# Byte addresses of TensorE's operands, and attention by pairs of heads

## The chip, the cores and the metric

The kernel runs on one core of a Trainium2 chip. The time is that of one execution of the whole program on the device, in microseconds (us); lower is better. Three runs were timed, and one execution was profiled.

## The reference

Two transformer blocks over 256 tokens of width 1024, in float32. The first block has two layers, each with a half-step feed-forward (FFN, width 2816, SwiGLU), a mixer (gated convolution, pooling, attention) and another FFN; layer 0 runs also on 256 context tokens, so most of its products have 512 token columns. Its attention has 8 heads of 64:

```
def ffn_sublayer(x, m, i, g, w1, w2):
    return x + HALF_STEP * m[:, 3 * i + 2, None] * swiglu(mod_norm(x, m, i, g), w1, w2)
...
s = jnp.concatenate([s_loc.reshape(B, NA_HEADS, nj, NA_QC, n_loc), s_ctx], axis=-1)
p = jax.nn.softmax(s, axis=-1).astype(v.dtype)
```

An image token attends to a neighbourhood among the 256 image tokens and to all 256 context tokens (512 scores a row); a context token to the 256 context tokens alone. The second block has retention, a sparse attention of 8 heads of 64 (two branches: all tokens up to the query, and a few compressed ones), and a layer of 16,384 experts of which each token takes 16 for each of 8 heads.

## The kernel before

Everything is kept with features on the 128 partitions and tokens along the row. A weight matrix comes from memory in units of 128x1024 (`Stream`): SyncE loads a unit into a `raw` buffer, and `Stream.split` (L238 to L242) makes of it two float32r halves, high and low, in an `hl` buffer: ScalarE copies the high half, VectorE or GpSimd subtracts. The buffers are taken in turn: `hl0` to `hl3`, two more in the FFNs (`hm`), one more in the second block (`hx`). The activations are split too: `Hh` and `Hl`, and `G` (high and low) behind the gate. `mm3` (L284 to L286) then makes three matmuls for each 128x128 block: high weight by high activation, high by low, low by high. In each, TensorE loads the weight block (128 columns) and streams 512 or 256 token columns past it. In three places (`winv`, `win2r`, and `wup` at L1813) the roles are turned: `Hh` or `Hl` is loaded and 512 columns of the unit are streamed.

All of these tiles lie at fixed bytes of a partition, one after the other in the order in which `run` allocates them. The built program gives these addresses modulo 256 bytes: X, Hh, Hl, hl0 and hl1 stand at 128; G, hl2 and hl3 at 96; hm at 0; hx at 128. Two more buffers, cut from the second halves of Hh and Hl for the expert units, stand at 128. Steps from block to block within a tile are multiples of 256 bytes, so each of its blocks has the tile's address modulo 256.

Attention in the first block (`attention`, L1028) is a generator; an item is one kind of query (image x or context c), one head h and one block qt of 128 queries. `mixer` calls it after every second block column k of its projections in layer 0, and after every fourth in layer 1, so one step lies between 6 or 12 matmuls of L284 to L286. In a step, for an item i, it issues: the softmax of item i+2 (`soft`), the division of item i+1 (`scale`), the scores of item i+3 (`score`, L1043, one float32 matmul over the 64 partitions of the head: heads with even number on partitions 0 to 63, odd ones on 64 to 127), the transposes of item i (`trans`, L1074, blocks of 128) and the products with V of item i-1 (`pv`, L1088, 64 weight columns, so the output goes to 64 PSUM partitions: 0 to 63 for even heads, 64 to 127 for odd ones). A float32 matmul is two passes, and the trace counts each as one. TensorE takes its instructions in the order written, so this order decides which matmuls are next to each other. Before the first step three scores are issued in a row:

```
        for i in range(3):
            prep(i)
            score(i)
        soft(0)
```

The scores go to three PSUM banks in turn (`sb`). Layer 0 has 32 items, 16 x and 16 c, layer 1 has 16 x. The sparse attention of the second block (`nsa`, L1340 on) has the same pipeline with 16 items (j, g, qt): L1393 scores (two matmuls of 128 columns for qt 0, of 256 for qt 1), L1429 transposes, L1440 and L1443 products (three matmuls for qt 0, five for qt 1).

Of the kernel before, what the change touches and what calls it, by code (L numbers as in the profile page):

```python
# [26 lines left out]
NSA = 68  # L27
MIX_LINS = (8, 9, 0, 10, 4, 11, 2, 6, 7, 1, 5, 3), (8, 9, 6, 10, 7, 11, 0, 4, 2, 1, 5, 3)
# [149 lines left out]

class Stream:
# [45 lines left out]
    def split(self, upto):  # L225
        nc = self.nc
        while self.done < min(upto, len(self.units)):
# [45 lines left out]
class Build:  # L273
# [40 lines left out]
    def run(self):  # L314
# [12 lines left out]
        self.half = base.tile([P, 4], F32, name="halfc")  # L327
        self.sm = ctx.enter_context(tc.tile_pool(name="small", bufs=2))
# [7 lines left out]
        self.raws = [("r0", raw[0]), ("r1", raw[1]), ("r2", fbp.tile([P, 1024], F32, name="raw2"))]  # L336
        self.hls = [("h0", hl[0]), ("h1", hl[1])]
        self.hls += [(f"h{j}", fbp.tile([P, 2, 1024], F32R, name=f"hl{j}")) for j in (2, 3)]
# [71 lines left out]
    def mods_setup(self, mp):  # L410
        nc, I = self.nc, self.I
        self.mp = mp
        self.mall = mp.tile([P, 2, 2, 72], F32, name="mall", bufs=1)
# [88 lines left out]
    def more(self, pool, end, n=2, stagger=False):  # L502

        W = self.W
        self.nmore = getattr(self, "nmore", 0) + 1
        new = [(f"m{self.nmore}_{j}", pool.tile([P, 2, 1024], F32R, name=f"hm{self.nmore}_{j}", bufs=1)) for j in range(n)]
# [323 lines left out]
    def mixer(self, l, T):  # L830
# [4 lines left out]
        with tc.tile_pool(name=f"mix{l}", bufs=2) as p:  # L835
# [178 lines left out]
    def attention(self, l, p, C, Q, K, V, bias, items, T):  # L1014
# [6 lines left out]
        nbias = [0]  # L1021

# [14 lines left out]
        def score(i):  # L1037
            kind, h, qt = items[i]
            L = 512 if kind == "x" else 256
            pr = slice((h % 2) * 64, (h % 2) * 64 + 64)  # L1040
            q0 = (256 if kind == "c" else 0) + qt * P
            o = self.bank[sb[i % 3]][:, :L]
            nc.tensor.matmul(o, Q[pr, h // 2, q0:q0 + P], K[pr, h // 2, 512 - L:512], start=True, stop=True)  # L1043
            ps[i] = o

        def soft(i):
# [3 lines left out]
            pr = p.tile([P, 512], F32, name="pr", tag="pr", bufs=3)[:, :L]  # L1050
# [18 lines left out]
        def trans(i):  # L1069
# [5 lines left out]
            t = p.tile([P, 512], F32, name="pt", tag="pt")[:, :L]  # L1075
# [3 lines left out]
        def pv(i):  # L1079
            kind, h, qt = items[i]  # L1080
            L = 512 if kind == "x" else 256
            t = ps.pop(i)
            pr = slice((h % 2) * 64, (h % 2) * 64 + 64)
            q4 = (i // 4) % 2
            o = ot_b[pr, q4 * 256 + qt * P:q4 * 256 + (qt + 1) * P]
# [4 lines left out]
            if i % 4 == 3:  # L1090
# [5 lines left out]
        for i in range(3):  # L1096
            prep(i)
            score(i)
# [4 lines left out]
        scale(0)  # L1103
        yield
        for i in range(n + 1):
# [6 lines left out]
            if i + 3 < n:  # L1112
# [3 lines left out]
            if i >= 1:  # L1116
                pv(i - 1)
# [3 lines left out]
    def second_mix(self):  # L1121
        nc, tc, I, W = self.nc, self.tc, self.I, self.W
        T = S
        with tc.tile_pool(name="mix2", bufs=1) as p:
            Xc = self.X[:, 1].rearrange("p k t -> p (k t)")
            W.ring(W.done, self.raws + [("xr", Xc[:, 1024:])], self.hls + [("hx", p.tile([P, 2, 1024], F32R, name="hx"))])
# [10 lines left out]
            self.npts = [Xc[:, 1024:1536], Xc[:, 1536:2048]]  # L1137
# [30 lines left out]
            self.npts = [Xc[:, 1024:1536], Xc[:, 1536:2048]]  # L1168
# [182 lines left out]
    def nsa(self, p, C, NQ, KS, VT, GT, KC, VC):  # L1351
# [31 lines left out]
        items = [(j, g, qt) for j in range(4) for g in range(2) for qt in range(2)]  # L1383
# [3 lines left out]
        def score(i):  # L1387
            j, g, qt = items[i]
            gs = slice(g * 64, (g + 1) * 64)
            L = (qt + 1) * P  # L1390
            o = sc_b[i % 3].rearrange("p (b n) -> p b n", b=2)[:, :, :L]
            for b in range(2):
                nc.tensor.matmul(o[:, b], NQ[gs, j, qt * P:(qt + 1) * P], KS[gs, b, :L], start=True, stop=True)  # L1393
            ps[i] = o

        def soft(i):
# [4 lines left out]
            pr = p.tile([P, 2, S], F32, name="npr", tag="npr", bufs=3)  # L1401
# [21 lines left out]
        def trans(i):  # L1423
# [6 lines left out]
            t = self.npts[i % 2][:, :2 * nb * P]  # L1430
# [3 lines left out]
        def pv(i):  # L1434
            j, g, qt = items[i]
            t = ps.pop(i)
            gs = slice(g * 64, (g + 1) * 64)
            nb = qt + 1
            o = ot_b[gs, (j % 2) * 256 + qt * P:(j % 2) * 256 + (qt + 1) * P]
            nc.tensor.matmul(o, VC[:, g * 4 + j], ct[:, qt], start=True, stop=False)  # L1440
            for b in range(2):
                for c in range(nb):
                    nc.tensor.matmul(o, VT[:, c, b * P + g * 64:b * P + (g + 1) * 64], t[:, (b * nb + c) * P:(b * nb + c + 1) * P],  # L1443
                                     start=False, stop=b == 1 and c == nb - 1)
            if i % 4 == 3:
                self.split2(self.g_(S, 4 + j), ot_b[:, (j % 2) * 256:(j % 2) * 256 + 256])

        for i in range(3):
            score(i)
# [5 lines left out]
        scale(0)  # L1455
        nc.vector.tensor_copy(ct.rearrange("p a t -> p (a t)"), self.bank[2][:, :S])
        yield
        for i in range(n + 1):
# [4 lines left out]
            if i + 3 < n:  # L1463
# [3 lines left out]
            if i >= 1:  # L1467
                pv(i - 1)
# [396 lines left out]
```

## Time and profile before

| what | value |
|---|---|
| runs timed | 2790.57, 2792.04, 2790.3 us; median 2790.57 us |
| profiled execution | 2787.89 us, its span 2786.0 us |
| TensorE (PE) | busy 2721.2 us, 98% of the span, 15899 matmul passes |
| VectorE (DVE) | busy 1760.2 us, 63% |
| ScalarE (ACT) | busy 1103.4 us, 40% |
| GpSimd (POOL) | busy 506.5 us, 18% |
| mean granted TensorE clock | 0.993 of full speed |

The span goes from the first to the last instruction; 1.9 us of the execution lie around it. The end of a matmul in the trace is modelled and matmuls overlap: one of 512 columns is shown with 0.39 us, though the next starts 0.23 us later. So the time that a matmul costs is read here from its start to the start of the next.

### The profile page before, as it was taken

Reading aid. Unit: us, or ns where it says so; the run is one execution under the profiler, and the core shown is the slowest. Engines: PE = TensorE matmul, PEld = TensorE weight load, DVE = VectorE, ACT = ScalarE, POOL = GpSimd, SP = SyncE. Lnnn points to the kernel's source line nnn. Section 1 sums busy time; section 2 is a strip of 40 time slices with the busy share of each in tenths; the row PEclk is TensorE's granted clock in tenths of the full one; section 3 lists DMA queues with packets and bytes.
Section 4 is the critical chain, followed back from the end, with each engine's and each line's share of the span. In section 5 each row is a group of like instructions: output and inputs, shape, how many; then the busy total and the mean of one; then the engine's idle time right before and its main releaser. Section 6 shows DMA issues by size and latency. Waiting matters only on the chain. (4 is left out here: it accounts for less than half of the span.)

```text
span 2786.0 us, 40945 instructions
## 1 busy us (share of the span) xinstructions
PE 2721.2 (98%) x15899; PEld 2348.9 (84%) x15899; DVE 1760.2 (63%) x3389; ACT 1103.4 (40%) x1867; POOL 506.5 (18%) x284
## 2 busy tenths in 40 slices
PE   6999999999999999999999999998999999999998
PEld 4888888679888898888888999878999999988887
DVE  6777865456777555555545655866696566655555
ACT  5222224433222233222344544554444544444454
POOL 1000011011000010000121001232498666400000
PEclk9999999999999999999999999999999999999999
DMA  6555643124556535655433556523555444466664
GB/s 254 188 184 187 194 141 115 46 78 130 181 187 194 184 108 187 197 188 193 139 125 110 177 184 196 175 69 129 183 168 166 146 150 146 152 195 205 196 192 141
DMA packets 129476, 451.40 MB, mean 162 GB/s; under 512 B 16000, under 2 KB 21120, under 8 KB 127744
## 3 DMA queue, kind: packets, MB, share of 16 engines
q1 hardware_dynamic: 129280, 448.77, 50.3%
q8 instruction: 125, 2.05, 0.3%
q14 instruction: 71, 0.58, 0.1%
HBM read 446.35 MB, written 2.10 MB: 161 GB/s over the span
## 5 line engine op out<-in xcount | busy, mean ns | idle before, releaser
L284 PE MATMUL bank<-Hh,hl 128*128 128x256 f32 (+1 forms) x1968 | 662.9, 337 | 6.9 <-ACT Hh L643 5.1
L286 PE MATMUL bank<-Hh,hl 128*128 128x256 f32 (+1 forms) x1968 | 642.2, 326 | 2.7 <-POOL hl L240 2.7
L285 PE MATMUL bank<-Hl,hl 128*128 128x256 f32 (+1 forms) x1968 | 642.8, 327 | 1.7 <-DVE Hl L646 1.6
L238 ACT ACTIVATE hl<-raw 128x1024 fp32r<-128x1024 f32 (+1 forms) x401 | 410.7, 1040 | 280.0 <-PE bank L1813 83.8
L242 DVE TENSOR_TENSOR hl<-raw,hl 128x1024 fp32r<-128x1024 f32 (+1 forms) x316 | 380.7, 1214 | 184.4 <-ACT hl L238 183.5
L284 PEld LDWEIGHTS bank<-Hh,hl 128*128 128x128 f32 x1968 | 374.9, 190 | 51.3 <-issue 11.2
L286 PEld LDWEIGHTS bank<-Hh,hl 128*128 128x128 f32 x1968 | 375.2, 191 | 36.1 <-POOL hl L240 3.3
L285 PEld LDWEIGHTS bank<-Hl,hl 128*128 128x128 f32 x1968 | 375.6, 191 | 34.2 <-DVE Hl L646 2.7
L494 DVE SCALAR_TENSOR_TENSOR junk<-wm,cb 128x1024 bf16<-128x1024 f32 x272 | 332.0, 1220 | 12.0 <-ACT cb L500 8.7
L597 POOL TENSOR_TENSOR nacc<-nlast,nacc 128x256 f32<-128x256 f32 (+1 forms) x56 | 61.6, 1104 | 1343.0 <-issue 849.4
L240 POOL TENSOR_TENSOR hl<-raw,hl 128x1024 fp32r<-128x1024 f32 x85 | 214.6, 2528 | 173.4 <-ACT hl L238 173.3
L284 PE MATMUL bank<-G,hl 128*128 128x512 f32 (+1 forms) x673 | 228.9, 340 | 0.0
L285 PE MATMUL bank<-G,hl 128*128 128x512 f32 (+1 forms) x673 | 228.1, 339 | 0.0
L286 PE MATMUL bank<-G,hl 128*128 128x512 f32 (+1 forms) x673 | 227.9, 339 | 0.0
L310 ACT ACTIVATE G<-silu 128x512 fp32r<-128x512 f32 (+1 forms) x88 | 50.9, 579 | 413.6 <-DVE silu L783 413.6
L783 DVE TENSOR_TENSOR silu<-silu,bank 128x512 f32<-128x512 f32 (+1 forms) x88 | 54.6, 621 | 203.1 <-PE bank L286 197.8
L1813 PE MATMUL bank<-hl,Hh 128*128 128x512 f32 x768 | 179.4, 389 | 0.0
L284 PE MATMUL bank<-Hh,hm 128*128 128x512 f32 (+1 forms) x496 | 177.5, 358 | 0.0
L286 PE MATMUL bank<-Hh,hm 128*128 128x512 f32 (+1 forms) x496 | 177.2, 357 | 0.0
L285 PE MATMUL bank<-Hl,hm 128*128 128x512 f32 (+1 forms) x496 | 176.9, 357 | 0.0
L1813 PEld LDWEIGHTS bank<-hl,Hh 128*128 128x128 f32 x768 | 144.2, 188 | 29.9
L709 DVE SCALAR_TENSOR_TENSOR X<-bank,mall,X 128x256 f32<-128x256 f32 x192 | 84.5, 479 | 133.1 <-PE bank L286 133.0
(351 smaller groups left out, 5144.5 us busy)
## 6 DMA issues: line engine op xcount, KB each, us to landing
raw<-in_w_dram SPq DMA_DIRECT2D x208, 512.0 KB, 4.1
wm<-in_wmod_dram SPq DMA_DIRECT2D x128, 512.0 KB, 4.2
X<-in_wdn_dram SPq DMA_DIRECT2D x64, 512.0 KB, 3.6
raw<-in_wdn_dram SPq DMA_DIRECT2D x64, 512.0 KB, 3.6
X<-in_wup_dram SPq DMA_DIRECT2D x64, 512.0 KB, 3.5
raw<-in_wup_dram SPq DMA_DIRECT2D x64, 512.0 KB, 3.5
raw<-in_w_dram SPq DMA_DIRECT2D x64, 448.0 KB, 3.8
wm<-in_wada_dram SPq DMA_DIRECT2D x48, 512.0 KB, 4.5
```

Source lines behind the costliest of these rows:

```text
L238: nc.scalar.activation(hl[:, 0, :n], raw[:, :n], AF.Copy)
L240: nc.gpsimd.tensor_tensor(hl[:, 1, :n], raw[:, :n], hl[:, 0, :n].bitcast(F32), OP.subtract)
L242: nc.vector.tensor_tensor(hl[:, 1, :n], raw[:, :n], hl[:, 0, :n].bitcast(F32), OP.subtract)
L284: mm(o, wh, xh, start=start, stop=False)
L285: mm(o, wh, xl, start=False, stop=False)
L286: mm(o, wl, xh, start=False, stop=stop)
L310: nc.scalar.activation(dst[0], src, AF.Copy)
L494: nc.vector.scalar_tensor_tensor(junk, w, 1.0, self.cb[c], op0=OP.mult, op1=OP.mult, accum_out=o)
L597: self.nadd.tensor_tensor(acc, last, acc, OP.add)
L709: nc.vector.scalar_tensor_tensor(x, self.bank_(b, T, half), g[:, d:d + 1], x, op0=OP.mult, op1=OP.add)
L783: nc.vector.tensor_tensor(s, s, self.bank_(bb, T), OP.mult)
L1813: nc.tensor.matmul(acc[t][n], c[:, a, ts], u[:, b, n * 512:(n + 1) * 512], start=e == 0 and a + b == 0, stop=e == P - 1 and a == 1)
```

## The change

Nothing that is computed changes, and the number of matmul passes stays 15899. There are two parts.

**Addresses.** Unused gap tiles are allocated ahead of some buffers, and each hl buffer gets 2112 float32 instead of 2048 (64 more). Every hl, hm and hx buffer now begins at 96 modulo 256, and `split` puts the two halves of a unit there, or 8 floats (32 bytes) further, at 128, where `wide` says so. X, Hh, Hl and G all stand at 128. `wide` picks the units whose products have 512 columns: the FFN units of the first three FFNs, layer 0's projections and those of layer 1 over both token sets, `winv`, `win2r` and `wup`. The units of 256 columns stay at 96. The two buffers cut from Hh and Hl stay at 128.

By pairs of addresses (streamed operand / loaded operand, modulo 256), the two built programs have these numbers of float32r matmuls:

| columns | 128/128 | 128/96 | 128/0 | 96/128 | 96/0 | 96/96 |
|---|---|---|---|---|---|---|
| 512, before | 2843 | 1087 | 985 | 639 | 480 | 562 |
| 512, changed | 6586 | 9 | 0 | 0 | 0 | 0 |
| 256, before | 4164 | 956 | 502 | 486 | 427 | 523 |
| 256, changed | 2771 | 4224 | 0 | 60 | 0 | 2 |

**Attention by pairs.** Items are ordered with the two heads of a pair next to each other. `score` issues two heads at once, every second step; `pv` issues the products of two heads at once, every second step, alternating between them. There is one more transposed buffer (`pt`, `npts`) and a fourth probability buffer, made of `nacc`, `nlast` and two tiles. GpSimd and SyncE issue the same kinds of instructions in the same order as before.

```
+def wide(label):
...
+    if kind in ("w1", "w2"):
+        return label[1] < 3
+    if kind in ("winf", "wout"):
+        return label[1] == 0 or kind == "winf" and label[2] >= 12
+    return kind in ("winv", "win2r", "wup")
...
+                if hl.shape[-1] == SPLIT:
+                    o = 8 if wide(label) else 0
+                    hl = hl[:, o:o + 2048].rearrange("p (a n) -> p a n", a=2)
...
-        hl = [base.tile([P, 2, 1024], F32R, name=f"hl{j}") for j in range(2)]
+        base.tile([P, 56], F32, name="gap0")
+        hl = [base.tile([P, SPLIT], F32R, name=f"hl{j}") for j in range(2)]
...
-                    for h in (2 * j, 2 * j + 1):
-                        for qt in range(2):
+                    for qt in range(2):
+                        for h in (2 * j, 2 * j + 1):
...
         def score(i):
+            for i in (i, i + 1):
+                kind, h, qt = items[i]
...
+                nc.tensor.matmul(o, Q[pr, h // 2, q0:q0 + P], K[pr, h // 2, 512 - L:512], start=True, stop=True)
...
         def pv(i):
...
             for c in range(nch):
-                nc.tensor.matmul(o, V[:, 4 - nch + c, h * 64:(h + 1) * 64], t[:, c * P:(c + 1) * P],
-                                 start=c == 0, stop=c == nch - 1)
+                for a in range(2):
+                    o = ot_b[a * 64:(a + 1) * 64, q4 * 256 + qt * P:q4 * 256 + (qt + 1) * P]
+                    nc.tensor.matmul(o, V[:, 4 - nch + c, (h + a) * 64:(h + a + 1) * 64], ts[a][:, c * P:(c + 1) * P],
+                                     start=c == 0, stop=c == nch - 1)
...
-            if i + 3 < n:
+            if i % 2 == 1 and i + 3 < n:
                 score(i + 3)
             if i < n:
                 trans(i)
-            if i >= 1:
-                pv(i - 1)
+            if i % 2 == 0 and i >= 2:
+                pv(i - 2)
```

`nsa` gets the same edits: items (j, qt, g), scores of both g in turn, products of both g in turn.

On TensorE's queue in layer 0's attention, between the projection matmuls, two steps of image items stood like this before (hl is the split weight unit, con holds the identity, pr the probabilities, pt their transpose; rows of equal instructions are merged with their count):

```order
L1043 MATMUL bank_66<-K,Q 128x512
L1074 MATMUL bank_68<-con_78,pr 128x128 x2
L1088 MATMUL bank_69<-pt,V 64x128 x2
L284 MATMUL bank_63<-Hh,hl_77 128x512
L285 MATMUL bank_63<-Hl,hl_77 128x512
L286 MATMUL bank_63<-Hh,hl_77 128x512
L284 MATMUL bank_63<-Hh,hl_77 128x512
L285 MATMUL bank_63<-Hl,hl_77 128x512
L286 MATMUL bank_63<-Hh,hl_77 128x512
L1043 MATMUL bank_67<-K,Q 128x512
L1074 MATMUL bank_68<-con_78,pr 128x128 x2
L1088 MATMUL bank_69<-pt,V 64x128 x2
```

With the change the same place reads (L1064 is the score, L1095 the transpose, L1110 the product with V, L298 to L300 the projection; the tiles nlast and pr_3238 are probability buffers):

```order
L1064 MATMUL bank_70<-K,Q 128x512
L1064 MATMUL bank_66<-K,Q 128x512
L1095 MATMUL bank_68<-con_79,nlast 128x128 x2
L298 MATMUL bank_63<-Hh,hl_78 128x512
L299 MATMUL bank_63<-Hl,hl_78 128x512
L300 MATMUL bank_63<-Hh,hl_78 128x512
L298 MATMUL bank_63<-Hh,hl_78 128x512
L299 MATMUL bank_63<-Hl,hl_78 128x512
L300 MATMUL bank_63<-Hh,hl_78 128x512
L1095 MATMUL bank_68<-con_79,pr_3238 128x128 x2
L1110 MATMUL bank_69<-pt,V 64x128 x4
```

Both scores now stand in one step and all products in the next, where each step had one score and one item's products.

In the sparse attention of the second block, the scores and products of one item stood together in a step before (X holds the queries and the transposed probabilities, KS and VT the keys and values, ct and Y the compressed branch):

```order
L1393 MATMUL bank_67<-KS,X 128x256 x2
L1429 MATMUL bank_68<-con_78,npr 128x128 x2
L1440 MATMUL bank_69<-ct,Y_13007 64x128
L1443 MATMUL bank_69<-X,VT 64x128 x4
L284 MATMUL bank_63<-Hh,hl_89 128x256
```

With the change the products of two heads alternate, from the step after their second transpose (nacc is the third buffer of transposed probabilities):

```order
L1454 MATMUL bank_68<-con_79,npr 128x128 x2
L1466 MATMUL bank_69<-ct,Y_12968 64x128 x2
L1470 MATMUL bank_69<-nacc,VT 64x128
L1470 MATMUL bank_69<-X,VT 64x128
L1470 MATMUL bank_69<-nacc,VT 64x128
L1470 MATMUL bank_69<-X,VT 64x128
L1470 MATMUL bank_69<-nacc,VT 64x128
L1470 MATMUL bank_69<-X,VT 64x128
```

Neighbouring products now come from different buffers and go to different halves of the output partitions.

## Rows read from the trace of the kernel before

**Rows 1.** The page's busy time of TensorE, share of the span, passes.

```profile
PE 2721.2 (98%) x15899; PEld 2348.9 (84%) x15899; DVE 1760.2 (63%) x3389; ACT 1103.4 (40%) x1867; POOL 506.5 (18%) x284
```

**Rows 2.** Waits of TensorE: waiting line, releaser, us in total, times, longest.

```profile
PE bank L605 <- DVE nacc L597: 17.2, 1, 17.2
...
PE bank L939 <- ACT pt L1076: 0.9, 1, 0.9
```

**Rows 3.** TensorE in order of time (start, shown length), hm and hl units on Hh.

```profile
75.89 0.39 PE L284 MATMUL bank<-Hh,hm 128*128 128x512 f32 x1
...
81.47 0.39 PE L284 MATMUL bank<-Hh,hl 128*128 128x512 f32 x1
...
86.91 0.39 PE L284 MATMUL bank<-Hh,hl 128*128 128x512 f32 x1
...
92.36 0.39 PE L284 MATMUL bank<-Hh,hl 128*128 128x512 f32 x1
...
97.96 0.39 PE L284 MATMUL bank<-Hh,hl 128*128 128x512 f32 x1
```

**Rows 4.** TensorE in order of time, units of 512 columns on G.

```profile
153.60 0.40 PE L284 MATMUL bank<-G,hl 128*128 128x512 f32 x1
...
159.21 0.39 PE L284 MATMUL bank<-G,hl 128*128 128x512 f32 x1
...
164.67 0.39 PE L284 MATMUL bank<-G,hl 128*128 128x512 f32 x1
```

**Rows 5.** TensorE in order of time, units of 256 columns on Hh.

```profile
1706.32 0.28 PE L284 MATMUL bank<-Hh,hl 128*128 128x256 f32 x1
...
1709.19 0.28 PE L284 MATMUL bank<-Hh,hl 128*128 128x256 f32 x1
...
1711.99 0.28 PE L284 MATMUL bank<-Hh,hl 128*128 128x256 f32 x1
```

**Rows 6.** TensorE in order of time, one step of layer 0's attention.

```profile
495.35 0.40 PE L286 MATMUL bank<-Hh,hl 128*128 128x512 f32 x1
495.67 1.12 PE L1043 MATMUL bank<-K,Q 64*128 64x512 f32 x2
496.73 0.44 PE L1074 MATMUL bank<-con,pr 128*128 128x128 f32 x2
497.09 0.65 PE L1088 MATMUL bank<-pt,V 128*64 128x128 f32 x4
497.67 0.50 PE L284 MATMUL bank<-Hh,hl 128*128 128x512 f32 x1
498.01 0.39 PE L285 MATMUL bank<-Hl,hl 128*128 128x512 f32 x1
```

**Rows 7.** TensorE in order of time, a step with 256 scores and eight passes of V.

```profile
510.47 0.70 PE L1043 MATMUL bank<-K,Q 64*128 64x256 f32 x2
511.10 0.66 PE L1074 MATMUL bank<-con,pr 128*128 128x128 f32 x4
511.68 1.09 PE L1088 MATMUL bank<-pt,V 128*64 128x128 f32 x8
512.70 0.50 PE L284 MATMUL bank<-Hh,hl 128*128 128x512 f32 x1
```

**Rows 8.** TensorE in order of time, the three scores ahead of layer 0's attention.

```profile
469.08 1.98 PE L1043 MATMUL bank<-K,Q 64*128 64x512 f32 x6
471.00 0.50 PE L284 MATMUL bank<-Hh,hl 128*128 128x512 f32 x1
```

**Rows 9.** TensorE in order of time, products of 64 weight columns, two output halves.

```profile
1802.84 0.46 PE L1243 MATMUL bank<-wc,hid 128*64 128x64 f32 x8
1803.23 0.50 PE L1184 MATMUL bank<-hl,Hh 128*128 128x512 f32 x1
```

**Rows 10.** Stretches: length, busy time of PE, PEld, DVE, ACT, POOL (instructions), clock, DMA.

```profile
469.00:583.00 114.00, 113.78 (x527) 70.90 (x527) 53.59 (x167) 50.11 (x117) 15.30 (x18) 1.00 0.18 54
1820.00:1895.00 75.00, 72.72 (x478) 59.50 (x478) 48.08 (x170) 37.32 (x96) 23.95 (x12) 1.00 0.22 71
```

More of the change, by code (lines that the diff above doesn't have):

```diff
@@ L336, in run @@
         self.raws = [("r0", raw[0]), ("r1", raw[1]), ("r2", fbp.tile([P, 1024], F32, name="raw2"))]
+        fbp.tile([P, 56], F32, name="gap2")
         self.hls = [("h0", hl[0]), ("h1", hl[1])]
-        self.hls += [(f"h{j}", fbp.tile([P, 2, 1024], F32R, name=f"hl{j}")) for j in (2, 3)]
+        self.hls += [(f"h{j}", fbp.tile([P, SPLIT], F32R, name=f"hl{j}")) for j in (2, 3)]
         W = self.W
@@ L412, in mods_setup @@
         self.mp = mp
+        mp.tile([P, 24], F32, name="gap3", bufs=1)
         self.mall = mp.tile([P, 2, 2, 72], F32, name="mall", bufs=1)
@@ L505, in more @@
         self.nmore = getattr(self, "nmore", 0) + 1
-        new = [(f"m{self.nmore}_{j}", pool.tile([P, 2, 1024], F32R, name=f"hm{self.nmore}_{j}", bufs=1)) for j in range(n)]
+        new = [(f"m{self.nmore}_{j}", pool.tile([P, SPLIT], F32R, name=f"hm{self.nmore}_{j}", bufs=1)) for j in range(n)]
         e = W.index(*end)
@@ L1021, in attention @@
         nbias = [0]
+        prs = [self.nacc, self.nlast] + [p.tile([P, 512], F32, name=f"pr{j}", bufs=1) for j in range(2)]
         def prep(i):
@@ L1037, in score @@
         def score(i):
[L1038 to L1044, printed above, removed]
+            for i in (i, i + 1):
+                kind, h, qt = items[i]
+                L = 512 if kind == "x" else 256
+                pr = slice((h % 2) * 64, (h % 2) * 64 + 64)
+                q0 = (256 if kind == "c" else 0) + qt * P
+                o = self.bank[sb[i % 3]][:, :L]
+                nc.tensor.matmul(o, Q[pr, h // 2, q0:q0 + P], K[pr, h // 2, 512 - L:512], start=True, stop=True)
+                ps[i] = o
         def soft(i):
@@ L1097, in attention @@
             prep(i)
-            score(i)
+        score(0)
         soft(0)
@@ L1103, in attention @@
         scale(0)
+        score(2)
         yield
-        for i in range(n + 1):
+        for i in range(n + 2):
             if i + 4 < n:
@@ L1382, in nsa @@
         ct = p.tile([P, 2, P], F32, name="ct")
-        items = [(j, g, qt) for j in range(4) for g in range(2) for qt in range(2)]
+        items = [(j, g, qt) for j in range(4) for qt in range(2) for g in range(2)]
         n = len(items)
@@ L1387, in score @@
         def score(i):
-            j, g, qt = items[i]
-            gs = slice(g * 64, (g + 1) * 64)
+            j, _, qt = items[i]
             L = (qt + 1) * P
-            o = sc_b[i % 3].rearrange("p (b n) -> p b n", b=2)[:, :, :L]
+            for g in range(2):
+                ps[i + g] = sc_b[(i + g) % 3].rearrange("p (b n) -> p b n", b=2)[:, :, :L]
             for b in range(2):
-                nc.tensor.matmul(o[:, b], NQ[gs, j, qt * P:(qt + 1) * P], KS[gs, b, :L], start=True, stop=True)
-            ps[i] = o
+                for g in range(2):
+                    gs = slice(g * 64, (g + 1) * 64)
+                    nc.tensor.matmul(ps[i + g][:, b], NQ[gs, j, qt * P:(qt + 1) * P], KS[gs, b, :L], start=True, stop=True)
         def soft(i):
@@ L1455, in nsa @@
         scale(0)
+        score(2)
         nc.vector.tensor_copy(ct.rearrange("p a t -> p (a t)"), self.bank[2][:, :S])
         yield
-        for i in range(n + 1):
+        for i in range(n + 2):
             if i + 2 < n:
@@ L1462, in nsa @@
                 scale(i + 1)
-            if i + 3 < n:
+            if i % 2 == 1 and i + 3 < n:
                 score(i + 3)
@@ L1466, in nsa @@
                 trans(i)
-            if i >= 1:
-                pv(i - 1)
+            if i % 2 == 0 and i >= 2:
+                pv(i - 2)
             yield
```

44 lines of the change are left out of this document (23 added, 21 removed).

## The prediction

> **What bounds the kernel now.** I read the page first: TensorE is busy for 98% of the span [rows 1]. Then the list of waits: the longest wait of TensorE, 17.2 us, lies in the opening, and in the first block's attention I find no more than single short ones, such as 0.9 us for a transposed block [rows 2]. So TensorE's queue is the path that sets the end, nearly everywhere, and the change has to be priced in the distance from the start of one matmul to the start of the next. For that I read TensorE in order of time, in two kinds of places: where whole weight units follow each other and nothing but the buffer differs, and in single steps of attention.
>
> **Addresses, 512 columns.** Each unit is 24 matmuls. In rows 3 the buffers are, by the built program, hm (address 0), hl0 (128), hl1 (128), hl2 (96), and all stream Hh or Hl at 128. The reader is to see that the units take 81.47 - 75.89 = 5.58, 5.44, 5.45 and 5.60 us [rows 3]: with equal addresses 5.445, with 128/0 5.58, with 128/96 5.60. On G, which stands at 96, it is the other way round: hl1 at 128 takes 5.61 us, hl2 at 96 5.46 [rows 4]. So what counts is not the buffer but whether the two addresses agree, and a matmul of 512 columns gains 0.135 / 24 = 5.6 ns where 128/0 becomes 128/128, 6.5 ns from 128/96 and 6.3 ns from 96/128. For 96/0 I take 6 ns; no row shows it apart. By the table of the change: 985 x 5.6 + 1087 x 6.5 + 639 x 6.3 + 480 x 6 ns = 5.5 + 7.1 + 4.0 + 2.9 = 19.5 us.
>
> **Addresses, 256 columns.** Here equal addresses are the slow ones: hl1 at 128 on Hh takes 2.87 us for 24 matmuls, hl2 at 96 2.80 us [rows 5], 2.9 ns less for each. 1393 matmuls go from 128/128 to 128/96: 4.1 us. About 1875 others come to 128/96 from 128/0, 96/128, 96/0 and 96/96, which no row prices; they lie between no gain and the same 2.9 ns (5.5 us), and since equal addresses are among them I take 2 ns, 3.8 us. Together 7.9 us, and for both widths 27 us.
>
> TensorE: Matmul & The Clock Gate of the Trainium skill (Part 2, Step-by-step) says that TensorE reads the stationary and the streamed operand through two independent ports, so that loading the next weights takes no read bandwidth from the running matmul. By that rule addresses would be worth nothing, and the sum below would come out 27 us higher. The rows disagree, by 0.16 us in 5.45, and I go by them.
>
> **Attention: what a block of scores or products costs.** Streaming first. Two score passes of 512 columns take 1.06 us [rows 6], two of 256 columns 0.63 us [rows 7]; the difference, 0.43 us, is one pass of 512. Two passes are 0.86 us, so 0.20 us of the block is not streaming. Four passes of V take 0.58 us [rows 6], eight 1.02 [rows 7]: 0.11 a pass, and 0.14 us that is not. Around the blocks more is lost: the projection matmul ahead of the scores takes 0.32 us to the next start and not 0.23, the two transposes 0.36 and the four 0.58, so 0.14 us beyond 0.11 each (about 0.05 behind the scores and 0.09 ahead of V), and the projection behind V takes 0.34 us and not 0.23 [rows 6, 7]. So a block of scores loses 0.09 + 0.20 + 0.05 = 0.34 us beyond its streaming, and a block of V 0.09 + 0.14 + 0.11 = 0.34 us.
>
> **Fewer blocks.** Before, layer 0 has 30 blocks of scores (three of its 32 items share the first) and 32 of products, layer 1 and the sparse attention 14 and 16 each: 122. With the change each pair has one of each: 16 + 8 + 8 pairs, 64 blocks. 58 x 0.34 = 19.7 us.
>
> **Scores of two heads at once.** The two heads of a pair lie on different halves of the partitions. Rows 8 hold the one place where that already happens: six passes of 512 columns, heads 0, 0 and 1, take 1.92 us from start to next start [rows 8], where 6 x 0.43 + 0.20 would be 2.78. Four passes' streaming is 1.72, and with 0.20 that is 1.92: so the two passes of head 1 ran beside two of head 0 and cost nothing. With the change every pair does this, and half of the score streaming goes: 0.86 us for each of 16 image pairs, 0.43 for 8 context pairs, and in the sparse attention, where an item has four passes of 128 or of 256 columns, 0.43 and 0.86 for four pairs each: 13.8 + 3.4 + 5.2 = 22.4 us. The three openings that had it already take off 3 x 0.86 = 2.6: 19.8 us.
>
> **Products of two heads at once.** They differ in the output half. The trace of before never has two of these next to each other, but it has a like case: eight float32 passes of 64 columns, four to each output half, take 0.39 us [rows 9]. At 0.11 us for 128 columns they would need 8 x 0.055 + 0.14 = 0.58 us one after the other, and 0.36 two at a time. The bounds are thus nothing and half of the streaming; I take half, since 0.39 is nearest to it. Pairs save 8 x 0.11 = 0.88 us (image, 16), 0.44 (context, 8), 0.66 and 1.10 (sparse, four each): 14.1 + 3.5 + 2.6 + 4.4 = 24.6 us.
>
> Part 3 of the same page (What overlaps and what doesn't) says that matmuls start and end strictly in program order. By that rule the second pass of head 0 would have to start before the first of head 1, and a pair of scores would need three slots where I count two. The six passes of rows 8 would then take 5 x 0.43 + 0.20 = 2.35 us; they took 1.92, so the rows speak against it.
>
> **What is late next.** A step shrinks from about 4.2 us to 3.0, while VectorE and ScalarE do the same work in it. In layer 0 VectorE is busy for 53.6 us of 114 and ScalarE 50.1, in the sparse attention 48.1 and 37.3 of 75 [rows 10]. My terms take 30 us off the first and 16 off the second stretch, which leaves VectorE at 64% and 81%. That is cover, but not even: the second score of a pair needs the PSUM bank that the softmax of one step before has read, and behind a waiting score stand the transposes and the projections, on which every engine waits. I allow 6 us for waits of this kind, and for the places where TensorE today waits for GpSimd's split units and cannot use a faster matmul; the bounds are 0 and some 25 us, 0.8 us a pair. The fourth probability buffer and the third transposed one only add slack. Gap tiles cost nothing: no instruction touches them.
>
> **The sum.** 27.4 + 19.7 + 19.8 + 24.6 - 6 = 85.5 us. Against the profiled execution, 2787.9 - 85.5 = 2702.4 us; the median of the runs stands 2.7 us above that execution, so 2705 us, 3.1% faster.
>
> **The rivals.**
> 1. The products do not run beside each other, because 128 columns from two buffers are not the 64 of one small tile in rows 9: 24.6 us stay, 2730 us. For it: no row of this shape. Chance 0.08.
> 2. Passes start in program order after all: a pair of scores keeps three of four slots (sparse: five of eight), products nine of 16. It gives back 16 x 0.43 + 8 x 0.215 + 4 x 0.11 + 4 x 0.215 = 9.9 us and 32 x 0.11 = 3.5: 2718 us. Against it rows 8. Chance 0.05.
> 3. The addresses give nothing, since the differences belong to something else in these buffers: 2705 + 27 = 2732 us. Against it: rows 3 and 4 swap their order with the streamed tile. Chance 0.04. (It is what the rule on two ports would give.)
> 4. The softmax chain becomes the bound of attention, 10 to 25 us more in waits, 2715 to 2730 us. For it: VectorE at 81% of the sparse stretch. Chance 0.09.
> 5. Slower: each second score waits for VectorE in all 32 pairs. To take back 91 us it must wait 2.9 us each time, a whole step; it decides from the point where VectorE falls a full step behind. Against it: the wait of TensorE in rows 2 that belongs to attention is 0.9 us, and VectorE has a third of the sparse stretch and half of layer 0's free [rows 2, 10]. Chance 0.03, some 2800 us.
>
> The forecast itself has 0.69; 0.02 stays for no difference, where two or three of these meet.
>
> **How the numbers follow.** About 0.2% (5.6 us) is what a measurement of this kernel can tell from no change. Faster by more: everything but the fifth rival and the rest, 0.95; within: 0.02; slower: 0.03. The forecast's own range is 2695 to 2716: below, no waits (6 us), the unpriced 256-column matmuls at their upper end (1.7) and some 2 us for rounding in the 0.34; above, waits of 13 us and those matmuls at nothing (3.8). The range for 8 in 10 keeps about that lower end and reaches to the first and third rival: 2694 to 2732 us.
>
> **What the new profile would show.** Units of 24 matmuls of 512 columns all near 5.45 us, also on the hm buffers and on G; units of 256 columns near 2.80. A pair of image scores (four passes) 1.06 us from start to next start, the eight products of a context pair and the 16 of an image pair near 0.58 and 1.02 us. If the 16 take 1.9, rival 1 holds; if four score passes take 1.5, rival 2; if hm units still take 5.58, rival 3. Waits of TensorE for pr, pt or the score banks would show rival 4. The forecast is wrong as a whole if the steps of attention stay near 4 us, or if any float32r matmul has become slower at its new address.

## The result and the profile after

| | median us | runs |
|---|---|---|
| before | 2791.31 | 4, 2790.3 to 2792.11 |
| with the change | 2724.39 | 4, 2722.74 to 2727.15 |
| ratio | 0.9761 | 95% interval 0.9745 to 0.9778 |

The change saves 67 us, 2.4%; 85.5 were forecast. 2724 lies inside the range of 2694 to 2732 us and above the forecast's own range, which ended at 2716: it is where rival 4 stood. The profiled execution took 2724.21 us, its span 2722.3. First the line of the page that answers to [rows 1], then four rows of TensorE's list of waits, as in [rows 2]:

```profile
PE 2639.4 (97%) x15899; PEld 2312.6 (85%) x15899; DVE 1759.6 (65%) x3389; ACT 1102.2 (40%) x1867; POOL 507.7 (19%) x284
```

```profile
PE bank L957 <- ACT pt L1097: 4.4, 2, 3.1
...
PE bank L1454 <- ACT X L1456: 2.7, 3, 2.1
...
PE bank L1095 <- ACT pt L1097: 2.2, 3, 0.8
PE bank L1454 <- ACT nacc L1456: 2.2, 1, 2.2
```

All four stand in layer 1's and the sparse attention, but for one wait of 0.8 us of the third row, in layer 0 (L957 is the pooling product, which shares a PSUM bank with the transposes). Before, the list had 0.9 us there for L939, which is L957 now.

The prices themselves are right. TensorE of the changed kernel in order of time: an hm unit on Hh, the next one, an hl unit, then a unit on G and its successor, then two units of 256 columns:

```profile
72.10 0.39 PE L298 MATMUL bank<-Hh,hm 128*128 128x512 f32 x1
...
77.54 0.39 PE L298 MATMUL bank<-Hh,hm 128*128 128x512 f32 x1
...
82.98 0.39 PE L298 MATMUL bank<-Hh,hl 128*128 128x512 f32 x1
...
148.26 0.39 PE L298 MATMUL bank<-G,hl 128*128 128x512 f32 x1
...
153.70 0.39 PE L298 MATMUL bank<-G,hl 128*128 128x512 f32 x1
...
1650.79 0.28 PE L298 MATMUL bank<-Hh,hl 128*128 128x256 f32 x1
...
1653.58 0.28 PE L298 MATMUL bank<-Hh,hl 128*128 128x256 f32 x1
```

Each of these units of 512 columns takes 5.44 us, on hm and on G too, where [rows 3, 4] had 5.58 and 5.61; 256 columns take 2.79. And two places of layer 0's attention, in the same view, answer to [rows 6, 7]:

```profile
486.30 0.66 PE L1110 MATMUL bank<-pt,V 128*64 128x128 f32 x8
486.89 0.50 PE L298 MATMUL bank<-Hh,hl 128*128 128x512 f32 x1
...
488.48 1.13 PE L1064 MATMUL bank<-K,Q 64*128 64x512 f32 x4
489.54 0.44 PE L1095 MATMUL bank<-con,pr 128*128 128x128 f32 x2
489.73 0.48 PE L298 MATMUL bank<-Hh,hl 128*128 128x512 f32 x1
```

Four score passes of a pair take 1.06 us and eight products 0.59, as forecast; the 16 of an image pair take 1.02 (median of 16).

So where are the 19 us? The attentions as stretches from the first score to the last product (length, busy time of PE, PEld, DVE, ACT, POOL, granted clock, DMA share, GB/s), layer 0, layer 1, sparse:

```profile
464.60:558.30 93.70, 91.49 (x557) 62.33 (x556) 55.90 (x172) 49.93 (x119) 15.89 (x18) 1.00 0.24 71
1397.30:1460.10 62.80, 56.93 (x445) 45.15 (x444) 38.63 (x107) 33.58 (x69) 24.36 (x25) 0.95 0.38 114
1753.50:1831.10 77.60, 67.28 (x497) 55.51 (x497) 54.78 (x198) 40.90 (x109) 27.65 (x13) 0.95 0.25 82
```

| stretch | before us | after us | gain | forecast of the terms | TensorE idle before, after |
|---|---|---|---|---|---|
| layer 0 | 120.0 | 93.7 | 26.3 | 30.2 | 0.2, 2.2 |
| layer 1 | 71.5 | 62.8 | 8.7 | 17.8 | 1.0, 5.9 |
| sparse | 82.9 | 77.6 | 5.4 | 16.1 | 2.3, 10.3 |
| all else | 2485.2 | 2461.9 | 23.3 | 27.4 | 35.3, 38.6 |

(The forecast column splits the prediction's terms for blocks, scores and products by the pairs of each stretch; idle time is the sum of TensorE's gaps; all else goes from TensorE's first matmul to its last, so without the opening's 17.2 us. A wait of 2.8 us just ahead of the sparse attention's first score, as long before as after, counts there.) The attentions gain 40.3 us of 64.1, layer 1 half of what it should and the sparse one a third, though each block costs what it should.

**A wait of the sparse attention.** VectorE, GpSimd, ScalarE and TensorE in order of time:

```profile
1782.06 2.15 DVE L1187 TENSOR_TENSOR RQ<-rsrc,rtmp 128x256 f32<-128x256 f32 x1
1784.12 0.41 DVE L1430 CUSTOM_DVE_ANT_0 npr<-bank,con 128x256 f32<-128x256 f32 x1
...
1781.49 2.43 POOL L254 TENSOR_TENSOR hl<-raw,hl 128x1024 fp32r<-128x1024 f32 x1 [4.10 <-ACT hl L252]
...
1785.12 0.51 ACT L1434 ACTIVATE npr<-npr,nst 128x256 f32<-128x256 f32 x1 [3.71 <-DVE nst L1432]
...
1786.12 0.36 ACT L1456 ACTIVATE nacc<-bank 128x256 f32<-128x256 f32 x1
...
1786.54 0.66 PE L1454 MATMUL bank<-con,npr 128*128 128x128 f32 x4 [2.20 <-ACT nacc L1456]
```

A rotation of 0.43 us (its usual time) is held for 2.15 us, until GpSimd's split ends at 1783.9. The softmax behind it starts at 1784.12, its exponential on ScalarE a microsecond later, the copy behind that at 1786.12, and TensorE, which needs the copied bank, has stood idle for 2.20 us. Eight VectorE instructions of this stretch are held so, 13.6 us beyond their usual times in all; before the change there were eight too, 12.6 us, with less behind them. In VectorE's groups of the sparse attention before (busy us, mean ns), rotations of one kind and form show it:

```profile
L1163 DVE TENSOR_TENSOR RQ<-rsrc,rtmp 128x256 f32<-128x256 f32 x3 | 6.4, 2131 | 0.1
...
L1163 DVE TENSOR_TENSOR RK<-rsrc,rtmp 128x256 f32<-128x256 f32 x3 | 1.3, 426 | 0.1
```

**The wait of layer 1.** TensorE, VectorE, ScalarE in order of time:

```profile
1446.14 0.66 PE L1095 MATMUL bank<-con,nlast 128*128 128x128 f32 x4 [0.77 <-ACT pt L1097]
1449.93 1.19 PE L957 MATMUL bank<-sb,pw 128*128 128x256 f32 x2 [3.13 <-ACT pt L1097]
...
1446.39 0.42 DVE L325 TENSOR_TENSOR G<-bank,G 128x256 fp32r<-128x256 f32 x1 [1.05 <-ACT G L324]
...
1447.61 0.69 DVE L1074 CUSTOM_DVE_ANT_0 pr<-bank,bias 128x512 f32<-128x512 f32 x1
...
1448.53 0.72 ACT L1081 ACTIVATE pr<-pr,sst 128x512 f32<-128x512 f32 x1 [2.17 <-DVE sst L1080]
...
1449.25 0.58 ACT L1097 ACTIVATE pt<-bank 128x512 f32<-128x512 f32 x1
```

The same stretch by the microsecond (as the stretches above, the granted clock behind POOL):

```profile
1447.00:1448.00 1.00, 0.00 (x0) 0.00 (x0) 0.95 (x3) 0.00 (x0) 0.00 (x0) 1.00 0.01 4
1448.00:1449.00 1.00, 0.00 (x0) 0.00 (x0) 0.93 (x5) 0.47 (x1) 0.00 (x0) 0.50 0.00 0
...
1455.00:1456.00 1.00, 1.00 (x17) 0.83 (x14) 0.49 (x2) 0.44 (x2) 0.00 (x0) 1.00 0.77 217
```

VectorE and ScalarE each wait for the other, in order: split of the finished products, two pooling sums, softmax, exponential, copy. From the split at 1446.39 to the end of the copy at 1449.83 that takes 3.4 us, and a step of layer 1 now takes 3.05. TensorE stands idle, its granted clock falls from 1.00 to 0.50 (2.4 to 1.2 GHz), and from 1449.9 to some 1454.8 it works at half speed: another 2.4 us. Behind a wait of the sparse attention there are 3.4 us more at half clock (1823.5 to 1826.9, 1.7 us lost). (The sparse attention's first 5 us run at half clock too, as its first 6 did before.)

### The profile page after: what moved, and what is told of

It is laid out like the page before. It is cut to its first block, busy times and chain, and to the rows that moved or that the text cites. A ratio compares the mean times of both kernels' runs of the same rounds, so it can differ in the third digit from the quotient of the medians.

```text
span 2722.3 us, 40945 instructions
## 1 busy us (share of the span) xinstructions
PE 2639.4 (97%) x15899; PEld 2312.6 (85%) x15899; DVE 1759.6 (65%) x3389; ACT 1102.2 (40%) x1867; POOL 507.7 (19%) x284
## 5 line engine op out<-in xcount | busy, mean ns | idle before, releaser
L298 PE MATMUL bank<-Hh,hl 128*128 128x256 f32 (+1 forms) x1968 | 661.4, 336 | 9.4 <-ACT Hh L661 5.1
L300 PE MATMUL bank<-Hh,hl 128*128 128x256 f32 (+1 forms) x1968 | 639.9, 325 | 4.1 <-POOL hl L254 4.1
L298 PEld LDWEIGHTS bank<-Hh,hl 128*128 128x128 f32 x1968 | 375.8, 191 | 48.5 <-issue 7.7
L300 PEld LDWEIGHTS bank<-Hh,hl 128*128 128x128 f32 x1968 | 375.2, 191 | 35.2 <-POOL hl L254 4.9
L298 PE MATMUL bank<-G,hl 128*128 128x512 f32 (+1 forms) x673 | 227.6, 338 | 0.0
L300 PE MATMUL bank<-G,hl 128*128 128x512 f32 (+1 forms) x673 | 226.8, 337 | 0.0
L298 PE MATMUL bank<-Hh,hm 128*128 128x512 f32 (+1 forms) x496 | 175.5, 354 | 0.0
L300 PE MATMUL bank<-Hh,hm 128*128 128x512 f32 (+1 forms) x496 | 175.3, 353 | 0.0
```

Source lines behind the costliest of these rows:

```text
L298: mm(o, wh, xh, start=start, stop=False)
L300: mm(o, wl, xh, start=False, stop=stop)
```

## The experiments

Each ratio is to the kernel before on the same chip; the changed kernel has 0.9761, some 2723 us beside medians of before of 2789.35 to 2789.93. Intervals are 0.0013 to 0.0015 to either side (some 4 us); e12 was timed once.

### e1 and e2: each part alone

```
e1: attention, nsa as before; gap tiles, SPLIT and wide kept
e2: attention, nsa as changed; no gap tile, hl [P, 2, 1024], wide and SPLIT gone
```

> The addresses alone, attention as before. Theory W (every price of the prediction holds, and the 19 us that are missing are waits of TensorE for the softmax chain in layer 1's and the sparse attention): the addresses give their whole term, about 27 us (512 columns 19.5, 256 columns 7.4), so some 2764 us, and the waits of TensorE in the attention stretches stay what they were before. Theory P (a price was too high): the addresses give clearly less than 27 us, 2770 us or more, or the full 27 us and the pairs are at fault.

> The pairs alone, operands placed as before. Theory W: the two parts add up, so about 40 us faster than before, 2751 us, perhaps 1 or 2 us better, since slower matmuls between the blocks leave the softmax chain a little more time; scores of an image pair again take 1.06 us and 16 products 1.0 us. Theory P: the pairs are worth less than 40 us by themselves and the two parts need each other.

e1: 2765.3 us, 0.9911 [0.9896, 0.9926], 24.6 us saved; the attentions keep their lengths (119.9, 71.6, 82.7). e2: 2749.73 us, 0.986 [0.9845, 0.9875], 40 us; its attentions take 93.8, 64.0 and 77.6. The parts add up: 24.6 + 40 = 64.6, and both together 67. The addresses give nearly their term, the pairs 40 of 58. What is missing is in the pairs.

### e3: products head after head

```
-            for c in range(nch):
-                for a in range(2):
+            for a in range(2):
+                for c in range(nch):
```

(the same in `nsa`)

> The changed kernel with the products of a pair head after head instead of interleaved; nothing else. Theory W: interleaving lets two products run beside each other, so the 16 products of an image pair go back from 1.0 to about 1.9 us; 10.6 us come back in layer 0's attention, but in layer 1's and the sparse attention part of the 14 us only fills waits that are there anyway, so 14 to 20 us slower than the changed kernel, 2738 to 2744 us. Theory P (products gained little by the order): within 5 us of the changed kernel's 2724 us.

2732.11 us, 0.9792 [0.9778, 0.9805]: 9 us slower than the changed kernel, less than the 14 to 20 of theory W and more than the 5 of theory P. TensorE in order of time, an image pair:

```profile
474.20 1.58 PE L1110 MATMUL bank<-pt,V 128*64 128x128 f32 x16
475.71 0.50 PE L298 MATMUL bank<-Hh,hl 128*128 128x512 f32 x1
```

The 16 passes take 1.51 us, not 1.9: even issued head after head, some passes of the second head run beside the first's. Context pairs take 0.594 us against 0.588 interleaved. Over all, products take some 42 us here, 31 interleaved and 59 before. So of the 29 us saved, the interleaving itself gives nearly 12; the rest comes from putting the two heads into one block.

### e4: GpSimd's splits in quarters

```
-   nc.gpsimd.tensor_tensor(hl[:, 1, :n], raw[:, :n], ...)
+   m = n // 4 if label[0] in ("win2f", "win2r", "winf", "wout2") else n
+   for k in range(0, n, m):
+       nc.gpsimd.tensor_tensor(hl[:, 1, k:k + m], raw[:, k:k + m], ...)
```

> The changed kernel with each split that GpSimd does in these blocks cut into four instructions of 256 columns. In the sparse attention eight VectorE instructions of 0.43 us (or 0.17) take 1.6 to 2.6 us, each while GpSimd is in a split of 2.4 us, and end with it. Theory W with VectorE held by GpSimd as the cause: VectorE is let in between the quarters, the waits of TensorE in the sparse attention fall from about 14 us to some 7, and the kernel is 4 to 8 us faster than the changed one, 2716 to 2720 us. Rival: the chain is late by its own order of instructions, and the time stays within 2 us of 2724, or rises since four instructions cost GpSimd more than one.

2715.15 us, 0.9734 [0.9721, 0.9747], 8 us faster than the changed kernel. VectorE's groups in the sparse attention, changed kernel and this one (busy us, mean ns):

```profile
L1187 DVE TENSOR_TENSOR RQ<-rsrc,rtmp 128x256 f32<-128x256 f32 x3 | 6.4, 2146 | 0.1
```

```profile
L1189 DVE TENSOR_TENSOR RQ<-rsrc,rtmp 128x256 f32<-128x256 f32 x3 | 1.5, 506 | 0.1
...
L256 POOL TENSOR_TENSOR hl<-raw,hl 128x256 fp32r<-128x256 f32 x37 | 27.3, 768 | 27.5 <-ACT hl L252 23.8 <-PE bank L1456 3.6
```

(L1189 is L1187 of the changed kernel.) A split now takes GpSimd 2.8 to 3.1 us instead of 2.43, and no VectorE instruction of this stretch is held for more than some 0.5 us. TensorE's idle time in this attention falls from 10.3 to 6.3 us, its time at half clock from 8.5 to 3.4, its length from 77.6 to 70.8; layers 0 and 1 stay (93.8, 62.9). The hold is shown as the cause of 6.8 us. Layer 1 has two holds as well (divisions of 1.58 and 2.32 us where 0.49 is usual); both go, and its attention is no shorter. And the 2.8 us ahead of the sparse attention, where VectorE was held for 2 us, are gone too: e4 gains them, but since that wait was as long before the change, they are no part of what is missing.

The Trainium skill (SBUF — State Buffer, Who interferes with whom) states that a VectorE instruction with two SBUF inputs and a GpSimd instruction that reads SBUF exclude each other for the whole instruction. The rows agree: 0.43 us became 2.15, ending with a split of 2.43 us. Two of the eight held instructions have only one SBUF input (0.17 us became 1.60 and 2.17), which the sentence does not cover.

### e5: the copy ahead of the exponential

```
             if i % 2 == 1 and i + 3 < n:
                 score(i + 3)
             if i < n:
                 trans(i)
+            if i + 2 < n:
+                soft(i + 2)
+            if i + 1 < n:
+                scale(i + 1)
```

(and the two calls gone from the head of the step; the same in `nsa`, as in e6 and e7)

> The changed kernel with each step's transposes and the copy that reads them issued ahead of the next softmax, so that on ScalarE the copy no longer stands behind an exponential that waits for VectorE. The list of waits names this copy as what TensorE waits for in most of layer 1's attention. Theory C (the order on ScalarE makes TensorE wait): the waits for the copy in layer 1, 5.9 us, fall by 3 us or more, and with them most of the 4.5 us at half clock behind the longest; in all 3 to 7 us faster than the changed kernel, 2717 to 2721 us. Theory V (VectorE's chain is late, and the copy only comes last): the same waits stay under another name, within 2 us of 2724, or later, since each exponential now stands behind a copy.

2723.13 us, 0.9761 [0.9747, 0.9774]: nothing. Layer 1's waits:

```profile
PE bank L957 <- DVE sb L950: 4.7, 2, 3.0
PE bank L1095 <- DVE nlast L1087: 0.7, 1, 0.7
PE bank L1095 <- DVE pr L1087: 0.2, 1, 0.2
```

5.6 us instead of 5.9, now under VectorE's name. The copy that the list named was only the last link; theory C falls.

### e6: all of a pair in one step

```
+            if i % 2 == 1:
+                if i >= 3:
+                    pv(i - 3)
+                if i < n:
+                    trans(i - 1)
+                if i + 3 < n:
+                    score(i + 3)
+                if i < n:
+                    trans(i)
```

> The changed kernel with all of a pair's work on TensorE in every second step (products of the pair before, transposes of one head, scores, transposes of the other), so that the projection matmuls are interrupted once for a pair and not twice; softmax as it was. Theory W: an entry and a return of TensorE cost 0.09 to 0.2 us, 32 of them are saved, 3 to 6 us, and one head's transposes get a step more for their softmax, which takes 3 to 6 us off the waits: 6 to 12 us faster than the changed kernel, 2712 to 2718 us. Rival: both heads' transposes use one PSUM bank, so the second waits for the copy of the first in each of 32 pairs, about 0.3 us each, and nothing is gained, 2721 to 2727 us.

2756.28 us, 0.988 [0.9865, 0.9896], 33 us slower than the changed kernel, far outside both. Its first wait, over the whole program:

```profile
PE bank L1095 <- ACT pt L1097: 18.0, 16, 3.2
```

The rival's mechanism was right and its price too small: the second head's transposes wait for the copy of the first, which stands behind an exponential that waits for VectorE, 1.1 us a time and not 0.3; the sparse attention has 16.1 us more of the same in its own lines.

### e7: the two heads' scores apart

```
+                score(i + 3, (0,))
             if i < n:
                 trans(i)
+            if i % 2 == 1 and i + 3 < n:
+                score(i + 3, (1,))
```

> The changed kernel with the transposes between the two heads' scores, so that no score runs beside another; 29 of the 32 pairs lose it, three in the openings keep it. Theory W: the scores' streaming of two heads doubles (18 us over 29 pairs) and each pair has one change of kind more (about 0.2 us, 6 us); in layer 1's and the sparse attention a third to a half of it fills waits, so 12 to 20 us slower than the changed kernel, 2736 to 2744 us. Theory P (scores gain nothing from standing side by side): within 6 us of it.

2739.58 us, 0.9818 [0.9805, 0.9832], 16 us slower, as expected. Two passes of one head take 1.053 us, as the four of a pair do (1.060): the second head's scores cost nothing in the changed kernel. Scores take 22 us more here, and TensorE's idle time in the attentions falls from 18.4 to 9.9 us, which covers part of them.

### e8 to e10: what is asked for in the same step

```
e8:                 lambda: mean(slice(64, P), 2), rest,
+                   *([lambda: None] if T == 256 else []),
                    lambda: pool_mix(...)
e9: -    self.split2(dst, src)            in pv
    +    late.append((dst, src))
    +    while late: self.split2(*late.pop())   behind the next scale
e10: e4 + e8 + e9
```

> The changed kernel with the two pool products of the second block (which TensorE issues in the same step as VectorE's last operation for them, and which wait 1.3 and 3.1 us there, the second followed by 4.5 us at half clock) issued one step later. Theory V (in a step of 3.05 us VectorE's chain is late for what is asked for in the same step): these two waits go, and the stretch at half clock with them; 4 to 6 us faster than the changed kernel, 2718 to 2720 us. Rival (the whole chain is late): TensorE waits as long for the transposed probabilities a step later, 2722 to 2725 us.

> The changed kernel with the split of a pair's finished products (ScalarE, then VectorE) issued one step later, behind the next softmax. In the changed kernel VectorE stands idle for 1 to 1.5 us in front of this split, which waits for ScalarE behind an exponential and a copy, and the next softmax stands behind it. Theory V with this loop as a cause: waits of TensorE for transposed probabilities and their copies fall by 3 to 6 us over the three attention stretches, 2718 to 2721 us. Rival: VectorE has the slack for it, within 2 us of 2724.

> GpSimd's splits in quarters, the pool products a step later and the split of finished products a step later, all in one. If these three make the waits and each acts in another place, the gains add up: 8 us of the quarters, 4 to 6 and 3 to 6 us, so 2703 to 2709 us, which is where the prediction stood. Rival: the waits share one cause and what is left of it after the quarters is small, 2712 to 2716 us.

e8: 2722.5 us, 0.9762 [0.9748, 0.9775]. Layer 1's attention is 2.9 us shorter (59.9, granted clock 1.00 throughout), but its idle time stays (5.7 us), under the transposes and the pooling product: what it saves is the stretch at half clock, and the whole kernel shows no gain. e9: 2723.43 us, 0.9767 [0.9753, 0.978]: layer 0 takes 92.3 and layer 1 60.5 us, 3.7 less together, the whole again the same. The time outside the attentions varies by up to 6 us from profile to profile (2459.1 to 2464.9), so gains of this size are seen in the stretches and not in the total. e10: 2711.28 us, 0.9721 [0.9708, 0.9735], attentions of 92.4, 60.3 and 71.8 us: the fastest kernel measured, 12 us below the changed one, of which e4 alone gives 8. It misses the 2703 to 2709 of adding gains, and beats the rival's end by a little; the 4 us between e10 and e4 lie within their intervals, and layers 0 and 1 are 3.8 us shorter with e8 and e9 together, no more than with e9 alone.

### e11: TensorE cut off from the softmax

```
-  nc.tensor.transpose(pt_b[...], pr[:, c * P:(c + 1) * P], ident)
-  nc.scalar.activation(t, pt_b[:, :L], AF.Copy)
+  nc.tensor.transpose(pt_b[...], K[:, 0, c * P:(c + 1) * P], ident)
+  ps[i] = K[:, 0, :L]
```

(the same in `nsa`, with its keys; ScalarE's copies are left out, so the output is not attention's)

> The changed kernel with TensorE cut off from the softmax: transposes and products of both attentions read the key tiles, which are there early, in place of the probabilities, and the copies of the transposed blocks on ScalarE are left out; scores, softmax and every count of matmuls stay, so the output is not attention's. Only the score banks still tie TensorE to VectorE. Theory W (what is missing from the predicted gain is TensorE's waits for the softmax chain): 15 to 22 us faster than the changed kernel, 2702 to 2709 us, which is where the prediction stood; attention of layer 0 takes some 91 us, of layer 1 some 55, the sparse one 64 to 68. Theory P (prices too high): within 6 us of 2724.

2714.87 us, 0.9729 [0.9715, 0.9742], 8.5 us faster: between the theories. Layer 0 takes 90.9 us, as expected; layer 1 59.7 and the sparse attention 74.1, where 55 and 64 to 68 were. Waits of layer 1, then of the sparse attention (first two):

```profile
PE bank L957 <- DVE sb L950: 3.0, 1, 3.0
...
PE bank L1181 <- ACT rsrc L1177: 3.5, 4, 1.4
PE bank L1417 <- DVE ce L1391: 2.8, 1, 2.8
```

With no probability to wait for, TensorE waits for pooling sums and rotated queries (the 2.8 us for the compressed branch are those ahead of the stretch). So theory W fails as it was put: not the softmax chain alone is late. That VectorE's and ScalarE's queues are, with everything that stands in them, is what these names suggest.

### e12: eight addresses

```
-                    o = 8 if wide(label) else 0
+                    self.at = getattr(self, "at", -1) + 1
+                    o = 8 * (self.at % 8)
```

> The changed kernel with the weight units shifted in turn by 0, 8, 16, ... 56 floats, so that they lie at all eight multiples of 32 modulo 256, while the streamed Hh, Hl and G stay at 128; a table of TensorE's start-to-start times by address and width comes out of one run. Theory of the prediction: at 512 columns only the equal address (128) is fast, 227 ns a matmul, and every other one takes about 233; at 256 columns the equal one is the slow one, 119.7 ns, and 96 takes 117.0. What 32, 64, 160, 192 and 224 give is open: with a rule that knows only equal and unequal, all 117 to 118.5 and 233; with one that depends on the distance, a slope over the eight. The time of the whole is some 10 us above the changed kernel's, since most 512-column units lose 6 ns a matmul.

TensorE in order of time, units of 24 matmuls of 512 columns on Hh at 128; they stand at 32, 64, 96, 128, 160, 192 and 224, and the last row starts the next:

```profile
80.81 0.39 PE L299 MATMUL bank<-Hh,hl 128*128 128x512 f32 x1
...
86.42 0.40 PE L299 MATMUL bank<-Hh,hl 128*128 128x512 f32 x1
...
91.92 0.40 PE L299 MATMUL bank<-Hh,hl 128*128 128x512 f32 x1
...
97.52 0.39 PE L299 MATMUL bank<-Hh,hl 128*128 128x512 f32 x1
...
102.97 0.39 PE L299 MATMUL bank<-Hh,hm 128*128 128x512 f32 x1
...
108.56 0.40 PE L299 MATMUL bank<-Hh,hm 128*128 128x512 f32 x1
...
114.16 0.39 PE L299 MATMUL bank<-Hh,hl 128*128 128x512 f32 x1
...
119.77 0.40 PE L299 MATMUL bank<-Hh,hl 128*128 128x512 f32 x1
```

5.61, 5.50, 5.60, 5.45, 5.59, 5.60 and 5.61 us (5.60 at 0): the equal address is the fast one, and 64 lies between it and the rest. With 256 columns, units on Hh that follow each other take 2.81 us at 224, 2.84 at 0, 2.88 at 32, 2.82 at 64, 2.84 at 96 and 2.87 at 128. The changed kernel, with all such units at 96, has 2.79: the unit's own address alone does not set the time. No slope, but not just equal and unequal either. The span, 2754.4 us, is 32 above the changed kernel's; the 10 us expected were mis-worked: over the trace, matmuls of 512 columns take some 30 us more than in the changed kernel and those of 256 some 3.

## Why the prediction was right or wrong

**Direction, mechanism, addresses: right.** Equal addresses at 512 columns: all matmuls of this width save some 20 us (19.5 forecast); at 256 columns, without those next to a wait, some 7 (7.9). e1 alone gives 24.6 of the 27.4. Rival 3 is out. The Trainium skill (TensorE: Matmul & The Clock Gate, Part 2, Step-by-step) has two independent read ports for the stationary and the streamed operand. By that, as the prediction read it, rival 3 would hold; these 24.6 us disagree.

**Blocks, scores, products: right, by their rows.** An image pair without waits costs 5.73 us before and 3.33 now, 2.40 saved (0.86 + 0.88 + 0.68 = 2.42 forecast); a context pair 1.54 (1.55). The scores run beside each other (e7) and the products too: rivals 1 and 2 are out. The split between the terms was less sure than it looked: e3 shows that two heads' products in one block run partly side by side without interleaving. One sum was 0.4 us off: the sparse opening's third item has passes of 128 columns, so 0.43 us come off for it and not 0.86. The Trainium skill (TensorE: Matmul & The Clock Gate, Part 3, What overlaps and what doesn't) has matmuls start and end strictly in program order. Against that, which the prediction weighed, speaks e3 too: at 0.109 us a pass, eight products in strict order, the two tiles overlapping only where the heads meet, need 7 x 0.109 + 0.14 = 0.90 us, and they took 0.594.

**The term that failed: "I allow 6 us for waits".** It measured about 24 (64.1 - 40.3), just within the bound of 25 that it was given: 4 in layer 0, 9 in layer 1, 11 in the sparse attention. 14.9 of it is idle time that was not there before. The place was another too: the prediction named the second score's bank, but scores lost only 2.5 us, and transposes and the pooling product waited. These 2.5 us are scores of layers 0 and 1 that take longer than their clean times add up to (in a few pairs the two heads' passes run one after the other; in the longest, at 1399.96, the second head starts as VectorE's softmax has read its bank). 4.1 us were lost at half clock behind waits, and some 2 us I can't place. The 18 us above the allowance and 4 us of the addresses' term outside the attentions, where TensorE's idle time grew by 3.3, make 22: the distance between the profiled executions (85.5 forecast, 63.7 measured; by the medians 67). This is rival 4 as it was priced (2715 to 2730), with a chance of 0.09; of its mechanism, the softmax chain, e11 bears out a part, 8.5 us. That 2724 still lies in the wide range is owed to its upper end, which rivals 1 and 3 set: both are out, so there is luck in it.

Two steps behind that term were wrong. "VectorE at 64% and 81%" was taken as cover, but a share over a stretch says nothing of a step: in layer 1, for which no row was read, a chain through both engines took 3.4 us where a step has 3.05. And the 48.1 us that VectorE was busy in the sparse attention [rows 10] were read as work, while some 11 us of them were instructions held by GpSimd (seven of the eight lie in that stretch), visible in the trace before: rotations of 2.1 us beside equal ones of 0.43. Nor was attention's wait of 0.9 us [rows 2] the only one: in the sparse attention TensorE was idle for 2.3 us, 1.1 of them before a transpose that waited for a copy.

**What is shown of the cause, and what is open.** e4 shows GpSimd's hold as 6.8 us of the sparse attention's length, where 11 are missing; its edit was not run on the kernel before, where the hold may have cost something already. By asking for something a step later, e8 spares layer 1 the stretch at half clock (2.9 us shorter) and e9 takes 3.7 us off layers 0 and 1: both show in the lengths of the stretches of one profile and not in the total. e5 excludes the order on ScalarE. In e10 the attentions still take 14 us more than the terms alone would leave, with 12.0 us of idle time against 3.5 before; e11 shows that not even TensorE's freedom from the softmax removes this. That it is VectorE's and ScalarE's queue as a whole is argued from the names in those lists, and no run took all of that work away.

## What to carry to other kernels

When TensorE's share of a step is cut, lay the other engines' chain of one step, in their order of issue, beside the new length of the step; a mean over the stretch hides it. Before trusting an engine's busy time, look for instances of one instruction with two durations: the long ones are waiting, and a neighbour's instruction that ends with them says for whom. A list of waits names the last link; moving that link (e5) tells whether it is the cause. And where matmuls use different tiles of the array, put them next to each other first: much of the gain comes before any interleaving.

## What the runs showed of the hardware that was not expected

Sixteen passes of products, eight of one output half and then eight of the other, took 1.51 us, between 1.02 (interleaved) and the 1.9 that one after the other would need: some of the second eight ran beside the first. Weights at 64 under operands at 128 cost 5.50 us a unit, between 5.45 (equal) and 5.60 (the others). Four GpSimd instructions of 256 columns (2.8 to 3.1 us) instead of one of 1024 (2.43) made the kernel 8 us faster: VectorE's holds of 1.6 to 2.6 us fell to some 0.5 beyond the usual time.
